# A hybrid encoder step on one core: a planner's port model, weight rests in two pieces, and another order for the last loop

## The chip, the cores and the metric

The kernel runs on one core of one Trainium2 chip. The time is that of the device, in microseconds, from the first to the last activity of the program. TensorE (PE) multiplies, VectorE (DVE), ScalarE (ACT) and GpSimd (POOL) do the element work, and SyncE (SP) issues the DMAs. PEld is PE's loading of the stationary operand, which runs beside its multiplying.

## What is computed

One step of a one-layer encoder for a prompt of 512 rows and a sample of 32 rows, each 1024 wide, in fp32:

```python
z = rmsnorm(x, g_mix) @ w_in               # qa ka va ga | qb kb vb gb | qm gm | qi ki wi
qb, kb, qi, ki = rope(qb), rope(kb), rope(qi), rope(ki)
mk, mv = split(rmsnorm(mem, g_mem) @ w_mem_kv)
oa = band_attention(qa, ka, va, rel_bias)  # 6 heads x 64: own chunk of 64 and the 8 before
s  = sum_h(wi_h * relu(qi_h @ ki))         # indexer: 8 heads x 32, one key for all
ob = attention over the top-k keys by s    # 6 heads x 64, k = min(256, L // 4)
om = attention(qm, mk, mv)                 # 4 heads x 64, 256 memory rows
x  = x + concat(oa * silu(ga), ob * silu(gb), om * silu(gm)) @ w_out
y  = rmsnorm(x, g_final)
```

The sample attends to caches (512 rows for A, 1024 for B, 256 for M) and its own 32 rows. The outputs are y of both, and the new keys and values.

## The kernel before

**Three matmuls for one.** For fp32 accuracy each operand is split in a high part (`wh`, `xTh`, `oBh`), which ACT rounds, and the rest (`wl = raw - wh`, `xTl`, `oBl`); a product is three matmuls, h·wh, l·wh and h·wl. The sample's outputs `oS` hold both parts side by side in 64 columns, so for them two matmuls do.

**Weights.** `w_load` issues the DMAs of the tiles `raw` in four buffers. `w_split` (line 488) takes them one after the other: it lets ACT round `wh` and then GpSimd subtract `wl` in one instruction (VectorE for weights 0 and 2, `WV`). `wh` and `wl` have three buffers. A tile is 128 partitions by 512, 592 or 768 elements; there are 70 of them in the run. PE reads a tile's two (or three) slices of 128 input rows one after the other.

**The order.** No order is written out. The class `Line` (lines 47 to 250) keeps a clock for each engine: `cost()` prices an instruction, `op()` moves the clock of its engine on, and `port()` lets VectorE and GpSimd wait for each other where both would use the read port that they share. Generators (`yield`) name a time at which they want to go on; the one with the earliest time is run next, and what it issues goes into its engine's queue at that place. So the planner's model sets in which order each engine's instructions stand in the program, and the chip then runs each queue in that order. `Timed` wraps every instruction, so that all of them have the line L273 in the profile (L284 in the changed kernel): names of tiles tell them apart.

**Stages.** First the indexer's projection (`index_group`), while the inputs and weights come in; `norms` (line 686) computes 1/rms of each block of 128 rows (`rs`, by way of `ss`, and `r16 = rs / 16`), `i_done` (line 799) rotates the indexer's queries and keys and scales its weights `wI`. Then the indexer's scores and the top-k are done beside the projections, and attention beside and behind them. `load_tables` (line 763) scales the tables `cos64` and `sin64`, eight tiles of 128x64, by `rs`. `sample_rows` (line 533) makes the sample's rows; those of `kb` and `qb` are rotated by `rope` (line 781), three instructions each.

**The end.** `out_part` multiplies by `w_out`. In the last loop the output's columns come in two halves, c0 = 0 and c0 = 512; in each half the tiles follow in the order sample (`NT`, 4), 0, 1, 2, 3. In the second half tile 3 (`apart`) is made in two pieces of 256 columns in two PSUM banks. `residual` adds the bank to `xr` (twice for the sample, whose two parts stand in the bank's rows 0 to 31 and 32 to 63). `settle` (line 1683) squares each piece on ACT, keeps a running sum, computes the power on GpSimd after the last piece, scales the half c0 = 512 on VectorE and the half c0 = 0 on ACT (for tile 2, `NT - 2`, on VectorE too), and SP writes the tile out.

Of the kernel before, what the change touches and what calls it, by code (L numbers as in the profile page):

```python
# [46 lines left out]
class Line:  # L47
# [4 lines left out]
    def __init__(self):  # L52
        self.clk = dict.fromkeys(("PE", "DVE", "ACT", "POOL", "SP", "DMA"), 0.0)
        self.ready, self.used = {}, {}
        self.boxes = {}
        self.tables = {"exp": (AF.Exp, AF.Tanh)}
        self.table = None
        self.mode = None
        self.taken = []
        self.tasks = []  # L60
        self.seq = 0
        self.margin = 0.3
        self.time = 0.0
        self.window, self.busy, self.slow = 0.0, 0.0, True
        self.warm = None

    def cost(self, eng, op, outs, ins, kw):
# [23 lines left out]
        if eng == "ACT":  # L91
            t = 0.05 + 0.045 * bool(chip) + n / 1200.0 + (0.19 if "accum_out" in kw else 0)
            for table, fs in self.tables.items():
                if kw.get("func") in fs and self.table != table:
                    self.table = table
                    t += 1.3
            return t
        return 0.15 + n * (0.0034 if op == "tensor_scalar" else 0.0021)

# [66 lines left out]
    def port(self, eng, t, d):  # L166

        for s, end, by in self.taken:
            if by != eng and s <= t < end:
                t = end  # L170
        self.taken = [x for x in self.taken[-40:]] + [(t, t + d, eng)]
        return t
# [130 lines left out]
def hybrid_step(ctx: ExitStack, tc: tile.TileContext, a: dict):  # L303
# [82 lines left out]

    rs, r16, ss = (cp.tile([P, 8], F32, name=n) for n in ("rs", "r16", "ss"))
    normed = set()
# [21 lines left out]
    def f(t):  # L410
        return t.bitcast(F32)
# [76 lines left out]
    def w_split():  # L488
        at = {}
        for i in range(len(w_list)):  # L490
# [11 lines left out]
            yield line.at(wh) - 0.2  # L502
            tsub(V if i in WV else G, wl, raw, f(wh))
            split.append((wh, wl))
# [28 lines left out]
    def sample_rows(nm, n, p):  # L533
# [19 lines left out]
        if nm in ("kb", "qb"):  # L553
            rope(out.rearrange("p (h d) -> p h d", d=64), out, T, 6, 64, ctab["cos64S"], ctab["sin64S"], V)

# [130 lines left out]
    def norms():  # L686
        for i in range(NT + 1 + NM // P):
# [6 lines left out]
            yield line.at(ss[:n, i:i + 1]) - 0.2  # L694
            G.tensor_scalar(ss[:n, i:i + 1], ss[:n, i:i + 1], EPS, None, op0=ALU.add)
            G.tensor_tensor(rs[:n, i:i + 1], ss[:n, i:i + 1], nhalf[:n], op=ALU.pow)
            G.tensor_scalar(r16[:n, i:i + 1], rs[:n, i:i + 1], 1.0 / 16, None, op0=ALU.mult)
            normed.add(i)
# [64 lines left out]
    def load_tables(d):  # L763
# [4 lines left out]

        def scale():
            for t in range(NT):  # L770
                yield from line.wait(lambda: t in normed)
# [8 lines left out]

    def rope(out, src, rows, nh, d, cos, sin, eng=None):

# [5 lines left out]
        sv = sin.rearrange("p (s d) -> p s d", s=2).unsqueeze(1).broadcast_to([rows, nh, 2, h2])  # L788
        V.tensor_tensor(o2, v2, sv, op=ALU.mult)
        V.tensor_tensor(out, src.rearrange("p (h d) -> p h d", d=d), cos.unsqueeze(1).broadcast_to([rows, nh, d]),  # L790
                        op=ALU.mult)
# [7 lines left out]
    def i_done(t, acc):  # L799
# [4 lines left out]
        if t > 0:  # L804
            A.copy(wI[:, t, :], acc[:, 288:296])
        give(acc)
# [4 lines left out]
        if t > 0:  # L811
            for r in (rs, r16):
                G.tensor_scalar(wI[:, t, :], wI[:, t, :], r[:, t:t + 1], None, op0=ALU.mult)
        indexed.append(t)
# [874 lines left out]
    def settle(t, c0, n):  # L1689
# [11 lines left out]
        if c0 + n < D:  # L1701
            V.tensor_scalar(run, new, EPS if j == 0 else old, None, op0=ALU.add)
            return
# [4 lines left out]
        V.scalar_tensor_tensor(y[:rows, 512:D], y[:rows, 512:D], run, gf[:rows, 512:D], op0=ALU.mult, op1=ALU.mult)  # L1708
        if t == NT - 2:

# [5 lines left out]
    for c0 in range(0, D, 512):  # L1716
        line.run(out_part(((1, 3, 3, 0, 256), (1, 3, 3, 256, 256)), c0, 512, lambda t, c, n: line.spawn(settle(t, c, n)),
                          (NT, 0, 1, 2, 3), (NT - 1,) if c0 else ()))
    while line.tasks:
# [66 lines left out]
```

## Time and profile before

| what | value |
|---|---|
| time, median of 3 runs | 363.46 us (363.11 to 363.86) |
| time of the profiled execution | 362.68 us |
| its span | 360.6 us |
| mean granted clock of TensorE | 0.996 |
| PE / PEld busy | 350.7 / 320.0 us |
| DVE / ACT / POOL busy | 276.6 / 219.6 / 191.0 us |

The span goes from the first to the last activity that the profiler sees; 2.08 us of the profiled execution's time lie outside it. Most of PE's busy time is back to back matmuls: a matmul's row gives 0.28 us for 256 columns, while the next one starts 0.11 us later, since they overlap in the array. Busy shares of the other engines are averages over stages. The last matmul starts at 352.58 us; what follows it is the last tiles' addition, norm, scaling and write.

### The profile page before, as it was taken

Reading aid. Unit: us, or ns where it says so; the run is one execution under the profiler, and the core shown is the slowest. Engines: PE = TensorE matmul, PEld = TensorE weight load, DVE = VectorE, ACT = ScalarE, POOL = GpSimd, SP = SyncE. Lnnn points to the kernel's source line nnn. Section 1 sums busy time; section 2 is a strip of 40 time slices with the busy share of each in tenths; the row PEclk is TensorE's granted clock in tenths of the full one; section 3 lists DMA queues with packets and bytes.
Section 4 is the critical chain, followed back from the end, with each engine's and each line's share of the span. In section 5 each row is a group of like instructions: output and inputs, shape, how many; then the busy total and the mean of one; then the engine's idle time right before and its main releaser. Section 6 shows DMA issues by size and latency. Waiting matters only on the chain.

```text
span 360.6 us, 7941 instructions
## 1 busy us (share of the span) xinstructions
PE 350.7 (97%) x2961; PEld 320.0 (89%) x2961; DVE 276.6 (77%) x696; ACT 219.6 (61%) x521; POOL 191.0 (53%) x213
## 2 busy tenths in 40 slices
PE   8999999999999999999999999999999999999991
PEld 8989988999998989898699898999979878888991
DVE  3665977797888978888999885999868576866463
ACT  5856767896747775595856553217665665544443
POOL 1778983375465574148436464534597412140751
PEclk9999999999999999999999999999999999999998
DMA  7998351475493322531203250133489412000015
GB/s 251 362 362 264 97 176 58 126 202 147 119 293 119 88 52 62 182 90 44 90 3 87 88 166 20 51 108 115 128 294 362 133 45 104 2 2 2 0 40 209
DMA packets 41478, 46.35 MB, mean 129 GB/s; under 512 B 5184, under 2 KB 36544, under 8 KB 41440
## 3 DMA queue, kind: packets, MB, share of 16 engines
q1 hardware_dynamic: 41440, 45.85, 39.9%
q8 instruction: 23, 0.38, 0.4%
q14 instruction: 15, 0.12, 0.1%
HBM read 39.67 MB, written 6.16 MB: 127 GB/s over the span
## 4 chain that ended last, share of the span: by engine, by line
PE 89%; DVE 4%; DMA 2%; issue 1%; ACT 1%; POOL 1%; SPq 1%; POOLq 0%; ACTq 0%; DVEq 0%
PE bank L273 89%; DMA raw<-in_w_in_dram 2%; POOL ss L273 1%; DVE ysel L273 1%; ACT sq L273 1%; DVE xr L273 1%; SPq L273 1%; DVE z L273 1%; DVE m L273 0%; DVE xTl L273 0%; DVE gate L273 0%; ACT wh L273 0%; ACT xTh L273 0%; DVE o L273 0%; DVE pt L273 0%
## 5 line engine op out<-in xcount | busy, mean ns | idle before, releaser
L273 POOL TENSOR_TENSOR wl<-raw,wh 128x512 fp32r<-128x512 f32 (+2 forms) x68 | 110.0, 1622 | 78.2 <-ACT wh L273 74.4
L273 ACT ACTIVATE wh<-raw 128x512 fp32r<-128x512 f32 (+2 forms) x70 | 50.1, 719 | 33.1 <-issue 13.6
L273 PE MATMUL bank<-wh,xTh 128*128 128x384 f32 (+1 forms) x192 | 65.3, 340 | 0.0
L273 PE MATMUL bank<-wl,xTh 128*128 128x384 f32 (+1 forms) x192 | 63.3, 330 | 0.0
L273 PE MATMUL bank<-wh,xTl 128*128 128x384 f32 (+1 forms) x192 | 63.2, 329 | 0.1
L273 ACT ACTIVATE z<-z,st 128x256 f32<-128x256 f32 (+3 forms) x77 | 41.0, 550 | 21.0 <-DVE st L273 20.9
L273 PE MATMUL bank<-xTh,wh 128*128 128x272 f32 x208 | 46.3, 304 | 0.0
L273 PE MATMUL bank<-xTh,wl 128*128 128x272 f32 x208 | 43.0, 288 | 0.0
L273 PE MATMUL bank<-xTl,wh 128*128 128x272 f32 x208 | 43.0, 288 | 0.0
L273 PEld LDWEIGHTS bank<-wh,xTh 128*128 128x128 f32 x192 | 36.1, 188 | 2.3 <-issue 1.6
L273 PEld LDWEIGHTS bank<-wh,xTl 128*128 128x128 f32 x192 | 36.2, 189 | 0.4 <-DVE xTl L273 0.3
L273 PEld LDWEIGHTS bank<-wl,xTh 128*128 128x128 f32 x192 | 36.1, 188 | 0.2 <-POOL wl L273 0.2
L273 PEld LDWEIGHTS bank<-xTh,wh 128*128 128x128 f32 x208 | 32.7, 189 | 1.7 <-issue 0.8
L273 PEld LDWEIGHTS bank<-xTh,wl 128*128 128x128 f32 x208 | 32.6, 189 | 0.1
L273 PEld LDWEIGHTS bank<-xTl,wh 128*128 128x128 f32 x208 | 32.6, 188 | 0.0
L273 DVE MAX8 m<-ysel 128x8 f32<-128x256 f32 (+2 forms) x48 | 26.4, 549 | 0.0
L273 DVE MATCH_REPLACE8 ysel<-m,ysel 128x256 f32<-128x256 f32 (+2 forms) x48 | 26.1, 543 | 0.0
L273 PE MATMUL bank<-ident,z 128*128 128x128 f32 (+1 forms) x161 | 25.0, 273 | 0.0
L273 ACT COPY pt<-bank 128x512 f32<-128x512 f32 (+1 forms) x26 | 14.1, 543 | 14.3 <-PE bank L273 14.2
L273 DVE SCALAR_TENSOR_TENSOR ysel<-r,wI,ysel 128x256 f32<-128x256 f32 (+2 forms) x21 | 17.8, 849 | 6.0 <-ACT r L273 5.6
L273 POOL TENSOR_TENSOR oBl<-o,oBh 128x128 fp32r<-128x128 f32 (+1 forms) x9 | 4.9, 549 | 30.4 <-ACT oBh L273 30.4
L273 PEld LDWEIGHTS bank<-ident,z 128*128 128x128 f32 (+1 forms) x161 | 18.2, 140 | 2.5 <-issue 1.0
(307 smaller groups left out, 892.6 us busy)
## 6 DMA issues: line engine op xcount, KB each, us to landing
raw<-in_w_in_dram SPq DMA_DIRECT2D x20, 384.0 KB, 3.6
raw<-in_w_in_dram SPq DMA_DIRECT2D x26, 256.0 KB, 2.9
raw<-in_w_out_dram SPq DMA_DIRECT2D x8, 384.0 KB, 3.1
nat<-in_x_prompt_dram SPq DMA_DIRECT2D x4, 512.0 KB, 7.9
raw<-in_w_mem_kv_dram SPq DMA_DIRECT2D x8, 256.0 KB, 2.8
xr<-in_x_prompt_dram SPq DMA_DIRECT2D x4, 512.0 KB, 4.8
out_dram<-xr SPq DMA_DIRECT2D x4, 512.0 KB, 2.6
xr<-in_x_t_dram SPq DMA_DIRECT2D x3, 544.0 KB, 5.8
```

The source lines that it names most:

```text
L273: return fn(*args, **kw)
```

## The change

- The planner's `port()`: VectorE now waits for at most one GpSimd instruction, keeps the port if its next instruction follows within 0.02 us of the last, and pushes GpSimd's clock on. `cost()` prices GpSimd's memsets and its one-column instructions.
- `norms`: the addition of EPS goes from GpSimd to VectorE, `r16` falls away; `i_done` scales `wI` by one instruction with two multiplications in place of two, the 1/16 being folded in ACT's copy.
- `w_split`: `wl` is subtracted in two instructions of 256, 384 or 296 elements (the one slice of 128 rows each; three slices go in three).
- `sample_rows`: the rotation of the sample's `kb` and `qb` goes to GpSimd.
- `load_tables`: the eight scalings of `cos64` and `sin64` wait until more than one tile has been scored.
- The last loop: order 0, 1, 2, 3, sample; the sample instead of tile 3 in two pieces at the end; tile 3 instead of tile 2 has both halves scaled on VectorE; running sums after the first go to GpSimd.

```diff
@@ class Line, port()
         for s, end, by in self.taken:
-            if by != eng and s <= t < end:
+            if by != eng and s <= t < end and (eng == "POOL" or t > self.kept + 0.02):
                 t = end
+                if eng == "DVE":
+                    break
+        if eng == "DVE":
+            if self.clk["POOL"] > t:
+                self.clk["POOL"] += d
+            self.kept = t + d
...
@@ cost(), GpSimd
+        if op == "memset":
+            return 0.05 + n / 1000.0
+        if n == 1:
+            return 0.57 if kw.get("op") == ALU.pow else 0.22
...
@@ w_split()
-            tsub(V if i in WV else G, wl, raw, f(wh))
+            step = max(raw.shape[1] // 2, 1)
+            for k in range(0, raw.shape[1], step):
+                c = slice(k, k + step)
+                tsub(V if i in WV else G, wl[:, c], raw[:, c], f(wh)[:, c])
...
@@ sample_rows()
         if nm in ("kb", "qb"):
-            rope(out.rearrange("p (h d) -> p h d", d=64), out, T, 6, 64, ctab["cos64S"], ctab["sin64S"], V)
+            yield line.idle(V)
+            rope(out.rearrange("p (h d) -> p h d", d=64), out, T, 6, 64, ctab["cos64S"], ctab["sin64S"], G, G)
...
@@ norms()
-            G.tensor_scalar(ss[:n, i:i + 1], ss[:n, i:i + 1], EPS, None, op0=ALU.add)
+            V.tensor_scalar(ss[:n, i:i + 1], ss[:n, i:i + 1], EPS, None, op0=ALU.add)
             G.tensor_tensor(rs[:n, i:i + 1], ss[:n, i:i + 1], nhalf[:n], op=ALU.pow)
-            G.tensor_scalar(r16[:n, i:i + 1], rs[:n, i:i + 1], 1.0 / 16, None, op0=ALU.mult)
...
@@ load_tables()
         def scale():
+            yield from line.wait(lambda: count["scored"] > 1)
...
@@ rope(); `by` is VectorE unless given
-        V.tensor_tensor(o2, v2, sv, op=ALU.mult)
-        V.tensor_tensor(out, src.rearrange("p (h d) -> p h d", d=d), cos.unsqueeze(1).broadcast_to([rows, nh, d]),
+        by = by or V
+        by.tensor_tensor(o2, v2, sv, op=ALU.mult)
+        by.tensor_tensor(out, src.rearrange("p (h d) -> p h d", d=d), cos.unsqueeze(1).broadcast_to([rows, nh, d]),
...
@@ i_done()
-            A.copy(wI[:, t, :], acc[:, 288:296])
+            A.activation(wI[:, t, :], acc[:, 288:296], AF.Copy, scale=1.0 / 16)
...
-            for r in (rs, r16):
-                G.tensor_scalar(wI[:, t, :], wI[:, t, :], r[:, t:t + 1], None, op0=ALU.mult)
+            r = rs[:, t:t + 1]
+            G.tensor_scalar(wI[:, t, :], wI[:, t, :], r, r, op0=ALU.mult, op1=ALU.mult)
...
@@ settle()
         if c0 + n < D:
-            V.tensor_scalar(run, new, EPS if j == 0 else old, None, op0=ALU.add)
+            if j == 0:
+                V.tensor_scalar(run, new, EPS, None, op0=ALU.add)
+            else:
+                G.tensor_tensor(run, new, old, op=ALU.add)
             return
...
-        if t == NT - 2:
+        if t == NT - 1:
...
@@ the last loop
-                          (NT, 0, 1, 2, 3), (NT - 1,) if c0 else ()))
+                          (0, 1, 2, 3, NT), (NT,) if c0 else ()))
```

How the change moves instructions is seen in the engines' queues. First PE's queue at the end of the program, where before the first and the second piece of tile 3 meet (`bank_4902` and `bank_4913`; the numbers behind the names tell buffers apart):

```order
L273 MATMUL bank_4902<-wh_4435,oBh_3080 128x256
L273 MATMUL bank_4902<-wh_4435,oBl_3081 128x256
L273 MATMUL bank_4902<-wl_4436,oBh_3080 128x256
L273 MATMUL bank_4913<-wh_4737,oBh_3080 128x256
L273 MATMUL bank_4913<-wh_4737,oBl_3081 128x256
L273 MATMUL bank_4913<-wl_4738,oBh_3080 128x256
```

In the changed kernel PE's queue at the same place, where tile 3 (`bank_4941`) ends and the sample's first piece begins:

```order
L284 MATMUL bank_4941<-wh_4762,oBh_2977 128x256
L284 MATMUL bank_4941<-wh_4762,oBl_2978 128x256
L284 MATMUL bank_4941<-wl_4763,oBh_2977 128x256
L284 MATMUL bank_4967<-wh_4637,oS_74 64x256
L284 MATMUL bank_4967<-wl_4638,oS_74 64x256
```

Before, the program ended on 18 matmuls of tile 3's pieces; now it ends on 12 of the sample, six in `bank_4967` and six in `bank_4978`, which before stood behind tile 3 of the half c0 = 0.

VectorE's last instructions before (the additions of tile 2 and of the two pieces of tile 3, then the scalings; `ss` is the running sum):

```order
L273 TENSOR_TENSOR xr2_3719<-bank_4873,xr2_3719 128x512
L273 SCALAR_TENSOR_TENSOR xr1_3718<-xr1_3718,ss_4701,gf_4698 128x512
L273 TENSOR_TENSOR xr3_3720<-bank_4902,xr3_3720 128x256
L273 TENSOR_TENSOR xr3_3720<-bank_4913,xr3_3720 128x256
L273 SCALAR_TENSOR_TENSOR xr2_3719<-xr2_3719,ss_4701,gf_4698 128x512
L273 TENSOR_SCALAR xr2_3719<-xr2_3719,ss_4701 128x512
L273 TENSOR_SCALAR ss_4701<-ss_4701 128x1
L273 SCALAR_TENSOR_TENSOR xr3_3720<-xr3_3720,ss_4701,gf_4698 128x512
```

VectorE's last instructions now:

```order
L284 TENSOR_TENSOR xr2_3856<-bank_4918,xr2_3856 128x512
L284 SCALAR_TENSOR_TENSOR xr1_3855<-xr1_3855,ss_4760,gf_4757 128x512
L284 TENSOR_TENSOR xr3_3857<-bank_4941,xr3_3857 128x512
L284 TENSOR_TENSOR xrS_3858<-bank_4967,xrS_3858 32x256 x2
L284 SCALAR_TENSOR_TENSOR xr2_3856<-xr2_3856,ss_4760,gf_4757 128x512
L284 TENSOR_TENSOR xrS_3858<-bank_4978,xrS_3858 32x256 x2
L284 SCALAR_TENSOR_TENSOR xr3_3857<-xr3_3857,ss_4760,gf_4757 128x512
L284 TENSOR_SCALAR xr3_3857<-xr3_3857,ss_4760 128x512
L284 SCALAR_TENSOR_TENSOR xrS_3858<-xrS_3858,ss_4760,gf_4757 32x512
```

Tile 3 is now added whole and ahead of the sample's four additions, both its halves are scaled on VectorE ahead of the sample's last scaling, and no running sum stands among them.

On GpSimd, the end of the eight scalings of the tables, where they stood before, early in the program between two weights' rests (six more scalings stand ahead of these rows):

```order
L273 TENSOR_SCALAR cos64_120<-cos64_120,rs_76 128x64
L273 TENSOR_SCALAR sin64_122<-sin64_122,rs_76 128x64
L273 TENSOR_SCALAR ss_78<-ss_78 128x1
L273 TENSOR_TENSOR rs_76<-ss_78,nhalf_67 128x1
L273 TENSOR_SCALAR r16_77<-rs_76 128x1
L273 TENSOR_TENSOR wl_577<-raw_414,wh_576 128x768
```

The same end of the eight scalings in GpSimd's queue now, many weights later (again six more ahead of these rows, and a rest, `wl_1633`, ahead of those):

```order
L284 TENSOR_SCALAR cos64_119<-cos64_119,rs_76 128x64
L284 TENSOR_SCALAR sin64_121<-sin64_121,rs_76 128x64
L284 TENSOR_TENSOR tg_1692<-tg_1692,gate_1205 128x272
L284 TENSOR_TENSOR gate_1205<-tg_1692,gate_1205 128x272
L284 MEMSET nb_1596 64x2x64
L284 TENSOR_TENSOR wl_1718<-raw_1542,wh_1717 128x256 x2
L284 TENSOR_TENSOR wl_1795<-raw_1566,wh_1794 128x256 x2
```

The eight scalings have moved behind the rest `wl_1633`, a gate's two multiplications follow them, and the next rest, `wl_1718`, comes after these, in two instructions.

## Rows read from the trace of the kernel before

**Rows 1.** The page, part 1: busy time, share and instructions of each engine.
```profile
PE 350.7 (97%) x2961; PEld 320.0 (89%) x2961; DVE 276.6 (77%) x696; ACT 219.6 (61%) x521; POOL 191.0 (53%) x213
```

**Rows 2.** Busy time by stretch: length, engines (instructions), granted clock, DMA share, GB/s.
```profile
100.00:120.00 20.00, 20.00 (x171) 18.25 (x171) 17.41 (x59) 12.47 (x32) 12.34 (x15) 1.00 0.61 189
...
160.00:180.00 20.00, 19.61 (x186) 16.14 (x186) 18.07 (x56) 14.67 (x40) 12.82 (x13) 1.00 0.23 74
```

**Rows 3.** Waits from 160 to 182 us: who for whom, total, times, longest.
```profile
PEld bank L273 <- DVE st L273: 1.1, 2, 0.7
...
PEld bank L273 <- DVE bi_ok L273: 0.6, 1, 0.6
```

**Rows 4.** Timeline of the end: start, duration, engine, instruction, idle before it.
```profile
343.17 0.28 PE L273 MATMUL bank<-wh,oS 128*64 128x256 f32 x1
...
344.53 0.28 PE L273 MATMUL bank<-wh,oBh 128*128 128x256 f32 x1
...
352.58 0.28 PE L273 MATMUL bank<-wl,oBh 128*128 128x256 f32 x1
...
352.89 0.42 DVE L273 TENSOR_TENSOR xr<-bank,xr 128x256 f32<-128x256 f32 x1 [0.17 <-PE bank L273]
...
353.54 0.42 ACT L273 ACTIVATE sq<-xr 128x256 f32<-128x256 f32 x1
...
353.90 0.75 DVE L273 SCALAR_TENSOR_TENSOR xr<-xr,ss,gf 128x512 f32<-128x512 f32 x1 [0.59 <-POOL ss L273]
354.57 0.48 DVE L273 TENSOR_SCALAR xr<-xr,ss 128x512 f32<-128x512 f32 x1
354.97 0.21 DVE L273 TENSOR_SCALAR ss<-ss 128x1 f32<-128x1 f32 x1
...
355.59 0.55 POOL L273 TENSOR_TENSOR ss<-ss,nhalf 128x1 f32<-128x1 f32 x1
356.17 0.72 ACT L273 ACTIVATE xr<-xr,ss 128x512 f32<-128x512 f32 x1 [2.12 <-POOL ss L273]
```

**Rows 5.** Timeline, VectorE: the sample's two additions of one piece.
```profile
314.03 0.86 DVE L273 TENSOR_TENSOR xrS<-bank,xrS 32x256 f32<-32x256 f32 x2
```

**Rows 6.** DMAs of the last loop: KB each, us from issue to landing.
```profile
out_dram<-xr SPq DMA_DIRECT2D x4, 512.0 KB, 2.6
...
out_dram<-xrS SPq DMA_DIRECT2D x1, 128.0 KB, 2.0
```

**Rows 7.** Tile `out_dram`, the prompt's writes: ns min/median/max, first and last start.
```profile
L273 SPq DMA_DIRECT2D out_dram<-xr x4: 332/332/363, 350.2 to 357.0; - x4
```

**Rows 8.** GpSimd by line and form: count, busy us, mean ns, idle before.
```profile
L273 POOL TENSOR_TENSOR wl<-raw,wh 128x512 fp32r<-128x512 f32 x38 | 52.4, 1384 | 55.1 <-ACT wh L273 51.7 <-DVE oSt L273 2.1 <-DVE kl L273 1.3
L273 POOL TENSOR_TENSOR tg<-tg,gate 128x272 f32<-128x272 f32 x13 | 11.1, 857 | 3.5 <-ACT tg L273 3.5
...
L273 POOL TENSOR_TENSOR kb<-rt,kb 128x384 f32<-128x384 f32 x3 | 3.0, 1013 | 7.0 <-DVE kb L273 7.0
L273 POOL TENSOR_SCALAR cos<-cos,rs 128x64 f32<-128x64 f32 x4 | 3.0, 756 | 0.0
...
L273 POOL TENSOR_TENSOR oAl<-o,oAh 128x256 fp32r<-128x256 f32 x3 | 2.2, 739 | 11.1 <-ACT oAh L273 11.1
```

**Rows 9.** Timeline, VectorE, the rotation of the sample's keys.
```profile
234.51 0.55 DVE L273 TENSOR_TENSOR kbS<-kbS,cos64S 32x384 f32<-32x384 f32 x1
...
235.09 2.09 DVE L273 TENSOR_TENSOR kbS<-rt,kbS 32x384 f32<-32x384 f32 x1
```

**Rows 10.** Timeline of the start: a weight's rest, and the input's rests `xTl`.
```profile
9.46 1.48 POOL L273 TENSOR_TENSOR wl<-raw,wh 128x592 fp32r<-128x592 f32 x1 [3.92 <-ACT wh L273]
...
10.06 2.20 DVE L273 SCALAR_TENSOR_TENSOR xTl<-xr,g_mix,xTh 128x544 fp32r<-128x544 f32 x2 [0.76 <-ACT xTh L273]
...
10.89 1.52 POOL L273 TENSOR_TENSOR xF<-xr,g_mix 128x64 f32<-128x64 f32 x2
...
11.58 0.40 PE L273 MATMUL bank<-wh,xTl 128*128 128x296 f32 x1
```

More of the change, by code (lines that the diff above doesn't have):

```diff
@@ L58, in __init__ @@
         self.mode = None
-        self.taken = []
+        self.taken, self.kept = [], -1.0
         self.tasks = []
@@ L385, in hybrid_step @@
     m8 = cp.tile([P, 8], F32, name="m8")
-    rs, r16, ss = (cp.tile([P, 8], F32, name=n) for n in ("rs", "r16", "ss"))
+    rs, ss = (cp.tile([P, 8], F32, name=n) for n in ("rs", "ss"))
     normed = set()
@@ L779, in load_tables, with rope @@
             line.spawn(scale())
-    def rope(out, src, rows, nh, d, cos, sin, eng=None):
+    def rope(out, src, rows, nh, d, cos, sin, eng=None, by=None):
         h2 = d // 2
```

## The prediction

> **What bounds the kernel now.** I read the shares first, then the stretches, then the waits of PE, and the end of the timeline last. The reader is to see in [rows 1] that PE is busy for 350.7 of the span's 360.6 us, and GpSimd, on which most of the edits fall, for 191.0. The stretches of 20 us say the same more sharply: from 100 to 120 us PE is busy all of the time while GpSimd works for 12.34; from 160 to 180 us [rows 2] PE falls a little short. The waits of that place [rows 3] are those of PE's loads on VectorE, 1.1 us for `st` and 0.6 for `bi_ok`, together 1.7. A change that leaves PE's matmuls as they are (its queue has the same ones before and after) can win in three places only: in the chain behind the last matmul, in waits such as these 1.7 us, and in the start.
>
> **The end, removed and added.** Let E be the end of the last matmul, 352.58 + 0.28 = 352.86 us [rows 4]. Before, tile 3's second piece is added at 352.89 and squared at 353.54; then the running sum (354.97) stands on VectorE behind two scalings of tile 2 (353.90 for 0.75, 354.57 for 0.48). The power follows at 355.59, the scaling at 356.17 for 0.72, the write is issued at 357.0 [rows 7], lands 2.6 us later [rows 6], and the span ends 1.0 after that. In sum 360.6 - 352.86 = 7.74 us behind E.
>
> Now 12 matmuls of the sample stand last. The same 12 took 344.53 - 343.17 = 1.36 us [rows 4], so tile 3 ends at E - 1.36 and the sample's first piece at E - 0.68. On VectorE, by its new queue, the two additions of the first piece, 0.86 for both [rows 5], are done at E + 0.2; the scaling of tile 2 takes 0.67 (from 353.90 to the next row's 354.57), to E + 0.9; the two additions of the second piece end at E + 1.75; then tile 3's scalings, 0.67 and 0.48, run to E + 2.9. On ACT the square of the second piece takes the 0.42 of 256 columns, and the reading of its sum some 0.2 (an estimate: as the one-column row of 354.97), to E + 2.35. GpSimd needs about 0.3 for the last sum with its start and 0.55 for the power [rows 4], to E + 3.2. The two halves of the sample are then scaled side by side, 0.72 as in [rows 4], to E + 3.9, and the write is issued 0.1 later, as before (356.89 to 357.0). It lands after the 2.0 us of the same write in [rows 6], at E + 6.0, and 1.0 later the span ends: E + 7.0. Tile 3's own write is issued about E + 3.0 and lands, at 2.6, at E + 5.6, ahead of the sample's. So the end is shorter by 7.74 - 7.0 = **0.75 us**. If the sample's landing took the 2.6 of the larger writes, because tile 3's is still under way, 0.15 would be left; if the second piece's additions got in ahead of tile 2's scaling, 0.67 would come off the sample's chain, and tile 3's write, issued as late as E + 3.0, would set the end at E + 6.6: a gain of 1.1. I take 0.75, since the undisturbed rows give it.
>
> **Rests in pieces.** A rest of 128x512 took 1384 ns, an instruction of 128x256 of the same kind 739 [rows 8]: two pieces cost 2 x 739 - 1384 = 94 ns more. There are 76 more instructions, so GpSimd gets 76 x 0.094 = 7.1 us more to do; at the other end, were each a whole fixed cost like the 0.55 of a one-column power [rows 4], 42 us. Even that would bring GpSimd to 233 of 360. It is hidden by GpSimd's own waits for ACT's `wh`, 51.7 us for the 512 wide form alone [rows 8]; without that cover each weight would come 0.1 late. What a piece can give: VectorE's sum of the sample's keys took 2.09 us, where its product just before took 0.55 [rows 9], since it ran into a rest on GpSimd. Behind half a rest such a wait ends up to 1384 - 739 = 0.65 us earlier. I take half of one such gain among the results of VectorE that PE waits for [rows 3], **0.3 us**; the bounds are a gain of all 1.7 and a loss of the same size, for the whole order moves with the new model, and no row shows the new order.
>
> **The start.** Here the rest of 9.46 us holds the port until 10.94, the first of two `xTl` comes out behind it, and PE's matmul on that starts at 11.58 [rows 10]. In halves the port is free at 10.25 or so, 0.7 us earlier, and so much is the most that can come of it. But GpSimd's second half may then be late: the second `xTl` was not held up although GpSimd's `xF` had been waiting since 10.89 (both `xTl` were done 2.20 us after 10.06, at 12.26). If VectorE keeps the port in this way until both are done, the second half ends no sooner than about 12.3, which PE reads shortly behind 11.58: a loss of up to 0.7. I take 0, between ends of one size.
>
> By the Trainium skill, in "SBUF — State Buffer", section "Who interferes with whom", the shared port is an exclusive lock and the issue order decides who waits; GpSimd's half, ready before the second `xTl`, would come in between, and the sum would be up to 0.7 us lower than with the loss that the row suggests. The row does not agree with it: the `xF` that stood ready did not get in between the two.
>
> **The rest, at nothing.** Seven additions of EPS go to VectorE (0.21 each, as the running sum in [rows 4]), and GpSimd loses these, seven of `r16` and three of `wI`; PE meanwhile works on weights split earlier, and uncovered VectorE's part would be 1.5 us. The six rotations of the sample cost GpSimd at most 1013 ns each, the price of the four times taller form [rows 8], 6.1 us, and VectorE saves six of 0.55 [rows 9]; they stand well ahead of the attention that reads them, and uncovered they would cost 6.1 - 3.3 = 2.8 us. SP issues the same DMAs; the writes of the end go out in the order 0, 1, 2, 3, sample, and none waits for a later one.
>
> **Sum.** -0.75 - 0.3 + 0 = -1.05 us. Against the profiled execution: 362.68 - 1.05 = 361.6. That execution lies 0.78 below the median of the runs, and it is runs that are compared: 363.46 - 1.05 = **362.4 us**.
>
> **Rivals.** First, the new order also removes PE's waits. The model of the port is nearer to what [rows 9] and [rows 10] show, and short pieces let VectorE through; against it, `st` and `bi_ok` end chains of VectorE's own work. With all 1.7 us gone: 363.46 - 0.75 - 1.7 = 361.0 us. Chance 0.17.
>
> Second, the end's gain does not reach the end: the sample's write lands as late as a large one, or the start loses what the end wins, so that 0 to 0.2 us is left: 363.3 us. For it speaks that much of the margin is one landing's difference (2.6 to 2.0) and that VectorE has six instructions to do behind E where it had five. This is also the case that the change does not do what it says. Chance 0.20.
>
> Third, slower: the block of scalings on GpSimd. Eight scalings at up to 756 ns [rows 8] are 6.0 us, and the gate's two multiplications behind them 2 x 0.86 = 1.7: the next rest stands 7.7 us behind the one ahead of it. PE uses up one of 70 weight tiles in 350.7 / 70 = 5.0 us. With two tiles in hand at that point nothing is seen (GpSimd has 7.7 us free in the 20 of [rows 2]); with one, PE waits 7.7 - 5.0 = 2.7 us: 363.46 - 0.75 + 2.7 = 365.4 us. It decides from the point where less than 7.7 us of PE's work is ready when the block starts. That there are three buffers for rests speaks against it; that GpSimd spends 51.7 us waiting for `wh` says that rests are not made long ahead. Chance 0.18.
>
> **How the numbers follow.** The forecast has 0.45, with its own range from 361.7 (1.1 at the end and 0.65 elsewhere) to 363.1 (little more than half of the end's 0.75 and nothing else). The range for all reaches from 360.3, the first rival with the most that the start can give, to 364.8, most of the way to the third: what is left out is 0.2, mostly above. About 0.2% (0.73 us) is what a measurement of this kernel can tell from no change: below 362.73 is faster, above 364.19 slower. Three quarters of the forecast and the first rival are faster, 0.34 + 0.17; a quarter of the forecast and most of the second are no change, 0.11 + 0.18; the third and the rest of the second are slower, 0.18 + 0.02.
>
> **What would show it.** In the new profile the span should end 7.0 us behind the last matmul's end, with the sample's write the last to be issued, some 4.0 us behind it. The matmul on the first `xTl` should start before 11.58 us, and a wait for `wl` may stand behind it. Near the eight scalings, wherever the trace shows them, PE should not wait for `wl`; if it does, the third rival has come in. The waits on `st` and `bi_ok` should add up to less than 1.7 us. The prediction is wrong if PE's back to back run is broken in a new place for more than a microsecond, or if the span ends over 7.6 us behind the last matmul.

## The result: slower by 0.65%, and the profile after

The changed kernel takes 365.6 us (median of 4 runs, 365.43 to 365.88), the kernel before 363.48; the ratio of the means is 1.0065 (95% interval 1.0053 to 1.0078). The forecast was 362.4 in a range from 360.3 to 364.8: the sign was wrong, and the time lies outside the range. The profiled execution took 365.43 us, with a span of 363.6 and a mean granted clock of 0.994.

The first line is part 1 of the changed kernel's page, the second its chain of waits by engine (part 4); the third is that chain in the kernel before.

```profile
PE 351.3 (97%) x2959; PEld 319.2 (88%) x2959; DVE 276.8 (76%) x701; ACT 219.3 (60%) x521; POOL 201.3 (55%) x274
...
PE 75%; DVE 14%; DMA 3%; ACT 3%; issue 2%; POOL 1%; SPq 1%; POOLq 0%; ACTq 0%; DVEq 0%
...
PE 89%; DVE 4%; DMA 2%; issue 1%; ACT 1%; POOL 1%; SPq 1%; POOLq 0%; ACTq 0%; DVEq 0%
```

Against [rows 1], PE's work and VectorE's are the same to 0.6 us, and GpSimd has 10.3 us more. But the chain that ends last runs over VectorE for 14% of the span, where it was 4% before: PE now waits. The stretches of 20 us say where (columns as in [rows 2]):

```profile
80.00:100.00 20.00, 19.05 (x148) 18.34 (x147) 18.24 (x48) 14.96 (x31) 13.15 (x17) 1.00 0.51 143
160.00:180.00 20.00, 20.00 (x193) 17.32 (x192) 15.56 (x52) 15.12 (x40) 11.46 (x15) 1.00 0.28 79
180.00:200.00 20.00, 19.42 (x143) 17.81 (x142) 18.72 (x47) 12.89 (x31) 12.95 (x15) 1.00 0.21 60
260.00:280.00 20.00, 18.82 (x166) 16.75 (x164) 18.41 (x42) 14.69 (x40) 10.11 (x14) 1.00 0.53 169
```

The gap of 160 to 180 us is gone, as hoped; three larger ones have come. PE's own waits (engine, for whom, us in total, times, longest) name them:

```profile
PE bank L284 <- POOL nhalf L284: 1.4, 1, 1.4
PE bank L284 <- ACT z L284: 1.1, 1, 1.1
PE bank L284 <- ACT bf_ok L284: 0.9, 1, 0.9
PE bank L284 <- DVE z L284: 0.6, 1, 0.6
PE bank L284 <- POOL wl L284: 0.5, 2, 0.3
PE bank L284 <- DVE ka L284: 0.2, 1, 0.2
PE bank L284 <- ACT wh L284: 0.2, 1, 0.2
```

The same view of before is shorter:

```profile
PE bank L273 <- POOL nhalf L273: 1.4, 1, 1.4
PE bank L273 <- ACT pt L273: 0.7, 2, 0.4
```

That is 2.1 us in all; here it is 4.9. The 2.8 more are most of what happened: the last matmul ends at 356.10 + 0.28 = 356.38 us, 3.52 later than in [rows 4].

The end, on the other hand, is shorter. Its timeline, as in [rows 4]:

```profile
356.10 0.28 PE L284 MATMUL bank<-wl,oS 128*64 128x256 f32 x1
...
356.51 0.73 DVE L284 SCALAR_TENSOR_TENSOR xr<-xr,ss,gf 128x512 f32<-128x512 f32 x1
...
357.27 0.86 DVE L284 TENSOR_TENSOR xrS<-bank,xrS 32x256 f32<-32x256 f32 x2
...
358.22 0.42 ACT L284 ACTIVATE sq<-xrS 32x256 f32<-32x256 f32 x1 [0.69 <-DVE xrS L284]
...
358.72 0.47 DVE L284 TENSOR_SCALAR xr<-xr,ss 128x512 f32<-128x512 f32 x1
358.87 0.36 POOL L284 TENSOR_TENSOR ss<-ss 32x1 f32<-32x1 f32 x1 [0.80 <-ACT sq L284]
359.31 0.54 POOL L284 TENSOR_TENSOR ss<-ss,nhalf 32x1 f32<-32x1 f32 x1
359.88 0.72 ACT L284 ACTIVATE xrS<-xrS,ss 32x512 f32<-32x512 f32 x1 [1.15 <-POOL ss L284]
...
360.69 0.33 SPq L284 DMA_DIRECT2D out_dram<-xrS  x1
```

The span ends 363.6 - 356.38 = 7.22 us behind the last matmul, 0.52 less than the 7.74 of before; 0.75 was forecast. So 3.52 - 0.52 = 3.0 us lie between the spans (363.6 and 360.6), and 2.1 between the medians. Of the 0.9 between these two numbers, 0.63 is that the profiled execution of before lies 0.80 below its median and that of the change 0.17. The rest is time outside the span: 2.08 us in the profiled execution of before, 1.83 in that of the change. This time goes with the kernel: it is 2.0 to 2.2 us on average in the kernel before, e2, e3, e5 and e8 below, and 1.8 in all others, and what sets it no run shows. So a difference of 0.3 us between two times may lie outside the program's work, and spans are given below where that matters (the median of the spans of before is 361.3 us, that of the change 363.85).

### The profile page after: what moved, and what is told of

The parts are those of the page before. It is cut to its first block, busy times and chain, and to the rows that moved or that the text cites. A ratio compares the mean times of both kernels' runs of the same rounds, so it can differ in the third digit from the quotient of the medians.

```text
span 363.6 us, 8046 instructions
## 1 busy us (share of the span) xinstructions
PE 351.3 (97%) x2959; PEld 319.2 (88%) x2959; DVE 276.8 (76%) x701; ACT 219.3 (60%) x521; POOL 201.3 (55%) x274
## 4 chain that ended last, share of the span: by engine, by line
PE 75%; DVE 14%; DMA 3%; ACT 3%; issue 2%; POOL 1%; SPq 1%; POOLq 0%; ACTq 0%; DVEq 0%
PE bank L284 75%; DMA raw<-in_w_in_dram 3%; DVE rank L284 3%; DVE z L284 1%; DVE rt L284 1%; ACT junk L284 1%; DVE junkS L284 1%; DVE rot L284 1%; DVE qb L284 1%; ACT wh L284 1%; DVE mTl L284 1%; SPq L284 1%; POOL wl L284 1%; POOL qb L284 1%; DVE xrS L284 1%
## 5 line engine op out<-in xcount | busy, mean ns | idle before, releaser
L284 POOL TENSOR_TENSOR wl<-raw,wh 128x256 fp32r<-128x256 f32 (+2 forms) x144 | 124.6, 889 | 99.5 <-ACT wh L284 96.2
L284 ACT COPY pt<-bank 128x512 f32<-128x512 f32 (+1 forms) x29 | 15.5, 537 | 17.1 <-PE bank L284 17.1
L284 DVE TENSOR_TENSOR xr<-bank,xr 128x256 f32<-128x256 f32 (+1 forms) x24 | 12.3, 512 | 14.0 <-PE bank L284 14.0
L284 ACT ACTIVATE junkS<-ysS,bi_neg 128x1056 int8<-128x1056 f32 x16 | 18.8, 1172 | 3.4 <-DVE bi_neg L284 3.4
```

The source lines that it names most:

```text
L284: return fn(*args, **kw)
```

## The experiments

Two theories stood after the result. **O**: the loss lies in the order of the instructions, which the planner makes anew. **I**: it lies in the new instructions themselves, GpSimd's longer work above all. Undoing one edit does not separate them, since each edit shifts the planner's clocks and with them the order of some thousand rows of PE's queue. So some kernels keep the order fixed: the planner is told of one set of instructions, and another is issued at the same places, by a switch in `Timed`:

```diff
-            self.line.op(self.name, op, outs, ins, kw)
+            if self.line.hush != "emit":
+                self.line.op(self.name, op, outs, ins, kw)
             kw.pop("func", None)
-            return fn(*args, **kw)
+            if self.line.hush != "plan":
+                return fn(*args, **kw)
```

With it PE's queue is the same, matmul for matmul. All times are medians of 5 to 12 runs beside runs of the kernel before on the same chip (medians of 363.32 to 363.41 us); a ratio is that of the means to before, with its 95% interval.

**e1 and e2: the old order with the new instructions, the new order with the old ones.** The switch stands around the rests, the EPS edit and the sample's rotations; the last loop and the place of the tables belong to the order here.

```diff
+            line.hush = "plan"
             tsub(V if i in WV else G, wl, raw, f(wh))
+            line.hush = "emit"
+            step = max(raw.shape[1] // 2, 1)
+            for k in range(0, raw.shape[1], step):
+                c = slice(k, k + step)
+                tsub(V if i in WV else G, wl[:, c], raw[:, c], f(wh)[:, c])
+            line.hush = None
```

Expected of e1: 

> The order of every queue is that of the kernel before; the instructions are those of the change (weights' rests in pieces, EPS on VectorE, no r16, wI in one instruction, the sample's rotations on GpSimd), each at the place of the one it replaces. The end is that of before. Theory O (the loss is the new order): 363.1 to 364.0 us, as before. Rival I (the loss is the instructions themselves, GpSimd's 10 us more and the rotations): 365.5 us or more, since the change had 365.6 with an end that its trace shows 0.5 shorter.

Expected of e2: 

> The order of every queue is that of the changed kernel, its end too; the instructions are the old ones (whole rests, EPS and r16 on GpSimd, wI in two, the sample's rotations on VectorE), each at the place of the new ones. Theory O: 365 to 367 us, PE's stops near 80, 182 and 262 us still there, as the new order makes them. Rival I: 362.5 to 363.2 us, the time before less the shorter end.

Measured: e1 367.61 us (ratio to before 1.0118, 1.0094 to 1.0142), e2 365.09 (1.0063, 1.004 to 1.0087). Half of theory O holds: the new order is slow with the old instructions too, and the new instructions make it only 0.5 slower (0.85 by the medians of the spans, 363.0 and 363.85). Of PE's waits, e2 has that for `bf_ok` whole (0.9), those for VectorE's and ACT's `z` in part (0.4 and 0.3), and 0.9 for `ka`. The other half fails: in the old order the same instructions cost 4.2 us. In e1's profiled execution most of this is one place, GpSimd ahead of 242 us:

```profile
234.20 1.07 POOL L276 TENSOR_TENSOR rt<-kbS,sin64S 32x384 f32<-32x384 f32 x1 [1.83 <-DVE kbS L276]
...
239.76 1.34 POOL L276 TENSOR_TENSOR qbS<-rt,qbS 32x384 f32<-32x384 f32 x1
241.07 2.13 POOL L276 TENSOR_TENSOR wl<-raw,wh 128x384 fp32r<-128x384 f32 x2
...
242.11 0.44 PE L276 MATMUL bank<-wl,xTh 128*128 128x384 f32 x1 [1.98 <-POOL wl L276]
```

The six rotations run from 234.20 to 241.1 ahead of a rest, and PE waits 1.98 us for it (before, VectorE had them: [rows 9]). An edit costs what the order around it lets it cost.

**The clock behind a stop.** Part of e1's time, and most of the spread between executions of one kernel, goes with the granted clock of TensorE. Its mean was 0.992 to 0.997 in all executions of before, e5, e6, e11, e14 and the change; e1, e3, e9, e13, e16, e17 and some others also have executions with less, down to 0.986 in e1, and those are among the longest of their kernel. Two profiles show where it falls. The stretches below (columns as in [rows 2]) are from e1, from e17, and from e9, whose PE queue is the same as e17's:

```profile
243.40:246.40 3.00, 3.00 (x10) 3.00 (x11) 2.93 (x4) 0.00 (x0) 3.00 (x3) 0.50 0.43 109
...
50.00:53.00 3.00, 3.00 (x12) 2.63 (x10) 0.32 (x1) 1.85 (x4) 2.90 (x5) 0.50 0.77 270
...
50.00:53.00 3.00, 3.00 (x18) 2.78 (x18) 1.83 (x3) 1.93 (x6) 2.82 (x5) 1.00 0.77 240
```

In e1 PE had just stopped for 1.98 and 0.35 us, in e17 for 1.30, and then the clock is 0.50 (1.2 GHz) in the 3 us shown: e17's matmuls, 0.9 us behind e9's at 48 us, are 2.4 behind at 55. e9's profiled execution had a stop of 1.20 at the same place and kept 1.00 (2.4 GHz) behind it. So a like stop is dearer in some executions than in others. Where this matters, the executions with a mean of 0.993 or more are given by themselves; e1's two took 365.81 and 366.96.

**e3, e4, e12, e16: another order, nothing else.** `self.margin = 0.3` becomes 0.29 (e3) or 0.31 (e12) in the kernel before, 0.31 in the changed one (e4) and in e11 (e16). The instructions stay the same, their order does not.

Expected of e3: 

> The kernel before with nothing changed but the planner's margin, 0.29 for 0.30: the same instructions in another order. Theory O in its general form (any other order of this planner costs or gives a microsecond or two, by chance): off 363.5 by over 0.7 us, either way. In its special form (the new port model and the late tables make a worse order): 363.0 to 364.0 us.

Expected of e4: 

> The changed kernel with the planner's margin at 0.31 for 0.30: its instructions in another order by the same model. General form: off 365.6 by over 0.7 us. Special form: 365.0 to 366.2 us, with a DVE-bound stretch ahead of a stop of PE near 260 us as in the changed kernel.

Expected of e12: 

> The kernel before with the planner's margin at 0.31 for 0.30: the same instructions, a smaller part of the order changed than with 0.29. If any other order is worse than the one that was kept: 363.8 to 366 us. If 0.29 was an accident: 363.1 to 363.7.

Expected of e16: 

> The changed kernel with early tables and the planner's margin at 0.31 for 0.30: the same instructions in another order. If early tables are better as a rule: 363.2 to 364.2 us. If 363.59 was the chance of one order: off by 0.7 us or more, rather above.

Measured: e3 364.96 (1.0048, 1.003 to 1.0066) and e12 364.42 (1.004, 1.0024 to 1.0056), both slower than before; e4 364.55, a microsecond faster than the change; e16 366.99, 3.4 slower than e11. So a hundredth in a planning constant moves the time by 1.0 to 3.4 us, either way; with the executions at 0.993 or more alone it is 0.8 (e3, 364.21) to 2.9 (e16, 366.45). That is the size of the whole loss, and several times the effects that were forecast.

**e8 and e10: the planner's model alone, and the change without it.** The new `port()` and `cost()` in the kernel before, the old ones in the changed kernel (the hunk as in the change, forward and back).

Expected of e8: 

> The kernel before with the planner's new port() and cost() alone: the old instructions, the old end, the tables scaled early, in the order that the new model makes. If the model makes the worse order: 365 to 366 us. If any other order is worse than the one the kernel had (as with the margin at 0.29, 364.96): anything from 364 to 366, with PE's stops at other places than in the changed kernel. If the late tables or the changed lengths make the worse order: 363.0 to 363.9.

Expected of e10: 

> The changed kernel with the planner's old port() and cost(): all new instructions and rules, in the order that the old model makes of them. If the new model is what makes the change's order worse: 363 to 364 us. If any new order costs 1 to 2 us, by whichever stops it happens to have: 364 to 367 us, with the stops of PE at other places.

Measured: e8 370.62 (1.023, 1.0197 to 1.0262), e10 373.7 (1.0287, 1.0266 to 1.0308), both above all that was expected. In both profiled executions the clock falls to 0.50 as well, in e8 from 56.3 to 59.7 us and in e10 from 273.7 to 280.5, so not all of this is waiting. PE's longest waits in e8 are others than in the change (for `bf_ok` 1.8, for VectorE's `z` 1.7, for `KSs` 1.3), in e10 one of 4.2 for ACT's `z`. Neither model is shown to be good or bad by itself; the order that either makes for the other's instructions is worse than both whole kernels' orders, and why is not shown.

**e11, e13, e15: the late tables.** e11 is the change without its wait for `count["scored"]`; e13 keeps the change's order and issues the eight scalings early; e15 is e11 in its order with the sample's rotations on VectorE.

```diff
@@ e11
-            yield from line.wait(lambda: count["scored"] > 1)
@@ e13, in w_split(), once; scale() only plans
+            if line.early and all(t in normed for t in range(NT)):
+                line.early.clear()
+                line.hush = "emit"
+                for t in range(NT):
+                    for x in (ctab["cos64"][:, t, :], ctab["sin64"][:, t, :]):
+                        G.tensor_scalar(x, x, rs[:, t:t + 1], None, op0=ALU.mult)
+                line.hush = None
```

Expected of e11: 

> The changed kernel with the tables' eight scalings early again, as before; since this shifts the planner's clocks, the order behind them is another one. If the late block of scalings cost PE a wait: 364.5 us or less, the difference in the stretch from 105 to 130 us. By the trace of the change, where PE has no wait there: no gain from the block itself, and 364 to 367 us by the chance of the order.

Expected of e13: 

> The changed kernel, each queue in its own order, but for the eight scalings of the tables, which stand early in GpSimd's queue (behind the first weight whose norms are all known), as before the change. If the block's late place costs the time by itself (the third rival): 363.5 to 364.5 us. If the loss lies in the order of the other instructions that the late tables bring with them: 365.2 to 366 us, with PE's stops near 80, 182 and 262 us still there.

Expected of e15: 

> The changed kernel with early tables (363.59 us), its queues in that order, with the sample's six rotations back on VectorE. If the rotations on GpSimd cost by themselves, in any order (1.05 us in the change's order): 362.5 to 363.0 us. If they cost only where VectorE's stretch ends in a stop of PE, which this order no longer has: 363.4 to 363.8.

Measured: e11 363.59 (1.0001, 0.9993 to 1.001), as fast as before; of the change's waits, that for `bf_ok` is 0.3 and that for ACT's `z` is gone. But e13 took 369.79 (366.45 to 370.68), so the block's late place is not the cause: put back early in the same order, it costs more. Its profiled execution, 366.94, has the change's stops and one more at 48 us, of 1.5 for `ka`; matmul for matmul it is as far behind the change at 140 us as at 100, so nothing was won where the block had stood. That execution and one of 366.45 had a granted clock of 0.995 and more; the other four had 0.987 to 0.990 and took 369.58 to 370.68. e15 took 365.1, with a new wait of 1.4 for ACT's `pt` at 246 us.

**e7: the change's order, the rotations back on VectorE.** Only the sample's six instructions change their engine.

Expected: 

> The changed kernel in its own order, with the sample's six rotations emitted on VectorE at the same place of the program, in two groups near 244 and 250 us. If GpSimd's rotations hold up VectorE by the shared port more than they save (its stretch from 231 to 263 us, which ends in PE's stop at 261.7): the stop of 1.3 us shrinks to 0.6 or less, and 364.7 to 365.1 us. If the rotations do not matter there: 365.6; if VectorE's 3.3 us more are what counts: 366.5 or more.

Measured: 364.55 (1.0047, 1.0029 to 1.0065), 1.05 faster than the change, and the wait of 1.1 for ACT's `z` is gone from PE's list. So this part's own cost in the change's order is 1 us; the same edit gave 1.5 us away in e15's order.

**e5, e6, e9, e14: parts of the change in the old order.** The end alone (e5); the pieces alone (e6); pieces, EPS edit and end (e9); pieces and end (e14).

Expected of e5: 

> The kernel before with the change's last loop alone (order 0, 1, 2, 3, sample; sample in two pieces; tile 3's halves on VectorE; running sums on GpSimd); everything ahead of it stands as before. By the trace of the changed kernel, whose span ends 7.2 us behind the last matmul's end instead of 7.74: 362.9 us, a gain of 0.5. By the prediction: 362.7, a gain of 0.75. If the end's gain is not real (lost to where the last matmul ends): 363.4.

Expected of e6: 

> The kernel before in its own order, with the weights' rests subtracted in two or three instructions and nothing else. If the 4 us of the old order with all new instructions came from the sample's rotations ahead of a rest (their 2.9 us of PE waiting for a rest near 240 us): 363.4 to 364.4 us, with up to 0.5 lost at the start where PE waits for the second half. If the pieces themselves cost by GpSimd's longer work: 365 us or more.

Expected of e9: 

> The order of the kernel before, with the change's pieces of the rests, its EPS on VectorE, no r16, wI in one instruction, and its last loop; the sample's rotations stay on VectorE, the tables are scaled early. If these edits' own effects add (pieces -0.45, end -0.3, the EPS edit near 0): 362.4 to 362.9 us, faster than both kernels. If the EPS edit carries part of the 4 us of the old order with all new instructions: 364 us or more.

Expected of e14: 

> The order of the kernel before with the pieces of the rests and the new last loop, and nothing else of the change. If the two gains add (0.45 and 0.3): 362.5 to 362.9 us, faster than both kernels. If they don't: 363.0 to 363.5.

Measured: e5 363.12 (0.9996, 0.9987 to 1.0004), a gain of 0.3 that the runs don't tell from none (its spans are 0.4 shorter, 360.9); e6 362.95 (0.9985, 0.9976 to 0.9993), with spans 0.1 shorter, 361.2; e9 363.47 (1.0016, 0.9999 to 1.0032); and **e14 362.36 (0.997, 0.9959 to 0.9981), faster than both kernels**, with spans 0.75 shorter, 360.55. e9 and e14 differ by the EPS edit alone, and their medians by 1.1 us. Of this 0.7 is left where e9's clock was 0.993 or more (eight executions, median 363.1; all six of e14 are such); e9's other four took 364.99 to 365.24.

**e17 and e18: what the EPS edit runs into.** In e9 a pair of pieces on GpSimd holds up eight small products of VectorE (the rows are in the next section). e17 makes these of another kind; e18 takes the pieces back to whole rests.

```diff
@@ e17; the planner is told of the old ones; o is the part of wsel, one the identity
-            V.tensor_scalar(o, one, wS[:, h:h + 1], None, op0=ALU.mult)
+            V.scalar_tensor_tensor(o, one, wS[:, h:h + 1], one, op0=ALU.mult, op1=ALU.mult)
```

Expected of e17: 

> e9 with its eight products wsel as SCALAR_TENSOR_TENSOR (times the identity once more, which changes no value) in place of TENSOR_SCALAR, in the same order. If a TENSOR_SCALAR waits through both pieces while an instruction with two tensor inputs gets in between them: the eight take 3.6 us or less beside the pair (4.53 in e9), PE's wait of 1.2 for QS falls to 0.4 or less, and the time is 362.3 to 363.0 us. If the pair holds any VectorE instruction: 4.5 us for the eight, 363.3 to 363.7.

Expected of e18: 

> e9 with whole rests in place of pieces, in the same order (EPS edit and end remain). If a TENSOR_SCALAR waits through a pair as through a whole: the eight take 4.3 to 4.6 us as in e9, PE's wait for QS is again about 1.2, and the time is 363.5 to 364.2 us (e9 without the pieces' 0.45). If the pieces make the wait longer: the eight are done sooner by 0.2 us or more and the time is no higher than e9's 363.47.

Measured: e17 364.48 (1.0036, 1.0016 to 1.0055; 363.57 at a clock of 0.993 or more), the eight take 5.21 us and PE waits 1.3. The view of the tile `wsel` in e17 (ns, least, median and most):

```profile
L276 DVE SCALAR_TENSOR_TENSOR wsel<-ident,wS x8: 340/344/2605, 41.8 to 46.7; 32x128 f32<-32x128 f32 x8
```

One of the eight was held for some 2.3 us, the others took about 0.34 each: the kind of the instruction is not the reason. e18 363.58 (1.001, 0.9998 to 1.0021), the eight take 4.40 beside one whole rest, and PE waits 0.8: a pair holds VectorE about as long as a whole one.

## Why the prediction was wrong, point by point

**The step that failed** is the term for the new order, under "Rests in pieces": a gain of 0.3, with bounds of 1.7 either way "for the whole order moves with the new model, and no row shows the new order". The bounds came from the waits that the old order had. A new order has its own: e3, e12, e4 and e16 show 1.0 to 3.4 us for no change of an instruction at all, e8 and e10 over 7 for another model (the clock's fall included), and e2 has the change's order with the old instructions at 365.09. In the change's trace PE waits 2.8 us more than before, at the start and at three new stops, of which the third is the rotations' (e7). The waits of before bound what can be won, not what can be lost. The prediction's own sign of being wrong came, if only just: a stop of over a microsecond in a new place (1.11, at 262 us). The three stops of the change, with where they come from:

At 80 us PE waits 0.95 for `bf_ok`, behind a full queue of ACT:

```profile
81.58 0.16 PE L284 MATMUL bank<-bf_ok,over 128*128 128x1 bf16 x1 [0.95 <-ACT bf_ok L284]
```

e2, e7 and e13 have this stop too, at the same matmul, and so has e4, whose PE queue is the change's up to 105 us; in e11, whose queue differs from 54 us on, it is 0.3. The instructions, the rotations and the block don't touch it, the order ahead of it does.

At 182 us the rows show a wait that the new model denies. VectorE and GpSimd in the change:

```profile
180.85 1.98 POOL L284 TENSOR_TENSOR wl<-raw,wh 128x384 fp32r<-128x384 f32 x2
...
181.77 1.81 DVE L284 TENSOR_SCALAR z<-z,st 128x384 f32<-128x384 f32 x2
...
183.19 1.05 PE L284 MATMUL bank<-ident,z 128*128 128x128 f32 x6 [0.58 <-DVE z L284]
```

One such scaling undisturbed took 0.42, so two need some 0.8; they took 1.81, as they waited until both pieces were done at 182.83. `port()` now lets VectorE wait for one GpSimd instruction only.

At 262 us ACT's `z` is late, since VectorE has run without a break from 238 us and was held up in the middle. The change, GpSimd, VectorE, ACT and PE:

```profile
244.61 1.00 POOL L284 TENSOR_TENSOR qbS<-rt,qbS 32x384 f32<-32x384 f32 x1
244.89 2.96 DVE L284 TENSOR_SCALAR rank<-ysS,bf_t 128x528 f32<-128x528 f32 x1
245.57 1.98 POOL L284 TENSOR_TENSOR wl<-raw,wh 128x384 fp32r<-128x384 f32 x2
...
262.78 1.20 ACT L284 ACTIVATE z<-z,st 128x128 f32<-128x128 f32 x3 [2.32 <-DVE st L284]
263.23 0.84 PE L284 MATMUL bank<-ident,z 128*128 128x128 f32 x3 [1.11 <-ACT z L284]
```

The same instruction in e2, where the rotations are VectorE's:

```profile
249.39 0.48 DVE L287 TENSOR_SCALAR rank<-ysS,bf_t 128x528 f32<-128x528 f32 x1
```

It waited 2.5 us, through the rotation's last instruction and both pieces, done at 247.55. That the rotations "stand well ahead of the attention that reads them" was true of their results; that they hold up VectorE on the way was not in the sum. e7 prices it: 1.05 us.

**The EPS edit "at nothing".** Wrong in the old order: 0.7 us between e14 and e9 at a like clock, 1.1 between the medians. What it costs in the change's order no run shows. It made `rs` ready sooner, GpSimd's queue ran ahead, and a pair of pieces fell on eight small products of VectorE. In e14, where none falls on them:

```profile
43.50 2.33 DVE L276 TENSOR_SCALAR wsel<-ident,wS 32x128 f32<-32x128 f32 x8
```

In e9, with GpSimd's pair and PE's wait for what VectorE makes next:

```profile
41.57 4.53 DVE L276 TENSOR_SCALAR wsel<-ident,wS 32x128 f32<-32x128 f32 x8
...
42.87 1.98 POOL L276 TENSOR_TENSOR wl<-raw,wh 128x384 fp32r<-128x384 f32 x2
...
47.37 0.82 PE L276 MATMUL bank<-identR,stk 32*128 32x32 f32 x8 [1.20 <-DVE QS L276]
```

4.53 - 2.33 = 2.2 us: the pair's 1.98 and a little. (e14's PE waits 0.4 for `rs` instead, ten us earlier, so that 0.8 is left of the 1.2.) In e18 it is the same with a whole rest:

```profile
42.17 4.40 DVE L276 TENSOR_SCALAR wsel<-ident,wS 32x128 f32<-32x128 f32 x8
...
43.47 1.84 POOL L276 TENSOR_TENSOR wl<-raw,wh 128x768 fp32r<-128x768 f32 x1
```

The prediction had priced seven instructions on VectorE (1.5 us at most), not what an engine that is ready sooner then collides with.

**The pieces.** 0.3 was forecast for their own effect, and e6 is 0.45 faster in the old order. But 0.3 of this lies outside the span (2.08 us in before, 1.77 in e6), and the spans' medians differ by 0.1 (their means by 0.25). So the number came near by luck in part; a gain by the way that was forecast, results of VectorE that come to PE earlier, can be 0.1 to 0.25 us of it. VectorE itself is held up less: it is busy for 271.0 us in e6, where it was 276.6. Beside the EPS edit, e9 and e18 differ by 0.1. GpSimd's additional work was forecast at 7.1 us for the pieces and is 12.9 in e6 (203.9 for 191.0), as a piece of 256 took 811 ns on average and not 739. It is hidden as the sum had it: of PE's waits in e6 those for a rest are 0.2.

**The start.** Taken at 0, between 0.7 either way. The change's rows, which answer to [rows 10]:

```profile
10.05 2.07 POOL L284 TENSOR_TENSOR wl<-raw,wh 128x296 fp32r<-128x296 f32 x2 [4.16 <-ACT wh L284]
...
10.65 2.06 DVE L284 SCALAR_TENSOR_TENSOR xTl<-xr,g_mix,xTh 128x544 fp32r<-128x544 f32 x2 [0.59 <-ACT xTh L284]
...
12.18 0.40 PE L284 MATMUL bank<-wl,xTh 128*128 128x296 f32 x1 [0.26 <-POOL wl L284]
```

Both `xTl` are done at 12.71, 0.6 behind the pair's end, which is time for one of them: the first came in between the two pieces, at the cost of GpSimd's second, and the second waited until the pair was done. So VectorE did not keep the port until both were done. The prediction had taken that from the `xF` in [rows 10], which stand there as one row of two; singly, before the change, the first ended at 11.68, while the second `xTl` was still at work:

```profile
10.89 0.79 POOL L273 TENSOR_TENSOR xF<-xr,g_mix 128x64 f32<-128x64 f32 x1
...
11.45 0.81 DVE L273 SCALAR_TENSOR_TENSOR xTl<-xr,g_mix,xTh 128x544 fp32r<-128x544 f32 x1
```

So this row did not speak against GpSimd's coming in between. In the change PE waits twice for a rest, 0.5 in all; e6 and e14, with the same pieces at the start, have 0.2. No run contradicts the 0, and none shows it closely: of the first 20 us PE is busy for 17.92 in the change and 18.59 before, but e9 and e17, with the same instructions there, have 18.64 and 18.05.

**The end.** The right mechanism, a little too large: 0.52 in the change's trace, 0.4 between the spans of e5 and of before, 0.75 forecast. The additions and the square came as worked out (square done 2.35 us behind the last matmul's end). The mis-sized term is GpSimd's last sum: 0.36 beside VectorE's scaling of 0.47, and the power starts at 359.31, 0.3 later than forecast; the write lands in 1.9 us.

**The rivals.** The third came nearest in time, 365.4 for 365.6, by another way than it said. The block stood where it was expected, and PE did not wait for it:

```profile
112.04 1.42 POOL L284 TENSOR_TENSOR wl<-raw,wh 128x256 fp32r<-128x256 f32 x2 [1.76 <-ACT wh L284]
113.44 0.73 POOL L284 TENSOR_SCALAR cos<-cos,rs 128x64 f32<-128x64 f32 x1
...
118.35 0.99 POOL L284 TENSOR_TENSOR gate<-tg,gate 128x272 f32<-128x272 f32 x1
...
119.69 1.44 POOL L284 TENSOR_TENSOR wl<-raw,wh 128x256 fp32r<-128x256 f32 x2 [0.21 <-PE bank L284]
```

The two rests stand 6.2 us apart, and from 105 to 130 us PE waits for no rest. e13 takes the block away from there and does not get faster. That e11 gains 2.0 us by the early tables is the gain of another order, and e16 loses more again with the same early tables. The first rival was half right: the waits of [rows 3] are gone, and others took their place. The second is refuted by the end's trace.

## What to carry to other kernels

Where a planner makes the order, price an edit in two parts: its own effect at the old places, and a new draw of the order, whose size is found by moving a planning constant by a hundredth (here 1.0 to 3.4 us, against parts of 0.3 to 1). Keep the order fixed to learn which parts are good, then take only those: pieces and end, in the order that had been kept, gave 362.36 us. Before two medians are compared, look at the granted clock and the span of each execution: here the same stop of PE was dearer where the clock fell behind it, and 0.3 us lay outside the span. And of an instruction moved to GpSimd, or made ready sooner there, ask which of VectorE's instructions it will hold up, not only who reads its result.

## What the runs showed of the hardware that was not expected

An instruction cut in two on GpSimd did not let a waiting VectorE in between, at three places: near 45 us in e9, and near 182 and 245 us in the change, VectorE waited for both pieces. At the start of the change it did get in, with the first `xTl`; and where GpSimd's next instruction needs the one before it, too (at 250.01 us a scaling of `rank` took 1.32 and not 0.48, beside two rotations of 1.09). What tells these cases apart stays open: e17 rules out that it is the number of VectorE's inputs alone. In sum the pieces let VectorE through more often all the same, by the 5.6 us of busy time that it lost in e6. Whether a gap between the pieces would help was not tried.

The runs of e1, e13 and e17 lie 3.6, 4.2 and 3.7 us apart from lowest to highest, those of e14 0.9. Most of this goes with the granted clock, which in the profiles of e1 and e17 fell to 0.50 right behind a stop of PE. Why it falls in some executions and not in others with a like stop (e9's 1.20, e13's 1.53 in its profile) stays open.
